# Roll of an 8192 x 8192 matrix: 31 of 128 row blocks copied by GpSimd's DMA ring

## The chip, the cores and the metric

The kernel runs on one core of one Trainium2 chip. The metric is the device time of one execution in microseconds; the median of the runs is given. Profiles are of one execution each.

## The reference

```python
def setup_inputs():
    return {"x": np.random.randn(8192, 8192).astype(np.float32), "shift": 100}

def reference(x, shift):
    return np.roll(x, shift, axis=1)
```

Every row of 8192 floats is rotated to the right by 100 places: column c of the result is column c - 100 of the input, and the first 100 columns are the input's last 100. Nothing is computed; 268.44 MB are read and 268.44 MB written.

## The kernel before

With s = 100, the kernel sets a = 256 (100 rounded up to a multiple of 128, plus 128) and g = a - s = 156. It splits each row at column a.

**The body** (lines 34 to 43): columns 256 to 8191 of the result are copied straight from HBM to HBM, 7936 floats or 31,744 bytes from a row. The 8192 rows are 128 blocks of 64 rows, and a block is seen as 16 groups (`e`) of 4 rows (`j`). One DMA copies row j of all 16 groups, so each of the 16 DMA engines gets one row. SP issues j = 0 and 2, ACT issues j = 1 and 3. In the last 4 blocks every row is cut at column `mid` = 4224, the middle of its 7936 columns, so that two DMAs of half rows stand where one was. SP's and ACT's DMAs are the hardware queues 1 and 10 of the profile. Each issuer has at most 4 DMAs in flight: it waits for its fourth last.

**The head** (lines 60 to 80): the first 256 columns of the result, of which 100 wrap around, go through SBUF. There are 16 stages of 512 rows, 4 rows on each of 128 partitions. For each stage GpSimd issues three loads on its software ring (queue 0): `t`, 3 runs of 1 KB for each partition, which span the end of one row and the start of the next; `h` with 100 floats (the wrapped end of the fourth row); and `h` with 156 floats (the start of the first row). VectorE puts the parts of `t` in their places in `h` with two copies. All stages have buffers of their own (`bufs=n_st`), so no load waits for a buffer. After the loads of all 16 stages GpSimd issues the 16 stores of `h` (line 80), 512 KB each. GpSimd has at most 8 DMAs in flight: each issue waits until the one eight before it has landed.

The order is the program's own: each issuer goes through its DMAs in the order of the loops, and body and head touch different columns, so no wait stands between them.

Of the kernel before, what the change touches and what calls it, by code (L numbers as in the profile page):

```python
# [1 line left out]

# [4 lines left out]


@with_exitstack
def kernel(  # L10
    ctx: ExitStack,
    tc: tile.TileContext,
    x: bass.AP,
    shift: int,
    out: bass.AP,
):
    nc = tc.nc
    n_rows, n_cols = x.shape
    s = shift % n_cols
    a = -(-s // 128) * 128  # L20
    if 0 < a <= 384 and a + 128 <= n_cols:
        a += 128
    g = a - s
    P = nc.NUM_PARTITIONS
    engines = [nc.sync, nc.scalar]
    n_chunks = 16
    rows = n_rows // n_chunks

    xm = x.rearrange("(c e j) w -> c j e w", e=16, j=4)
    om = out.rearrange("(c e j) w -> c j e w", e=16, j=4)
    if a < n_cols:
        blocks = n_rows // 64
        mid = (a + n_cols) // 256 * 128
        for c in range(blocks):
            parts = ((a, mid), (mid, n_cols)) if c >= blocks - 4 and a < mid else ((a, n_cols),)  # L40
            for j in range(4):
                for lo, hi in parts:
                    engines[j % 2].dma_start(out=om[c, j, :, lo:hi], in_=xm[c, j, :, lo - s:hi - s])
    if a == 0:
        return


    if a > 512:
        for i in range(n_chunks):
            r = slice(i * rows, (i + 1) * rows)  # L50
            nc.gpsimd.dma_start(out=out[r, :s], in_=x[r, n_cols - s:])
            if g > 0:
                nc.gpsimd.dma_start(out=out[r, s:a], in_=x[r, :g])
        return

    Q = 4  # L60
    n_st = n_rows // (P * Q)
    reads = ctx.enter_context(tc.tile_pool(name="reads", bufs=n_st))
    heads = ctx.enter_context(tc.tile_pool(name="heads", bufs=n_st))
    xt = x.rearrange("(k p q) c -> k p q c", q=Q, p=P)
    ot = out.rearrange("(k p q) c -> k p q c", q=Q, p=P)
    tiles = []
    for k in range(n_st):
        t = reads.tile([P, Q - 1, a], x.dtype)
        h = heads.tile([P, Q, a], x.dtype)
        lead = bass.AP(tensor=x.tensor, offset=(k * P * Q + 1) * n_cols - s,  # L70
                       ap=[[Q * n_cols, P], [n_cols, Q - 1], [1, a]])
        nc.gpsimd.dma_start(out=t[:], in_=lead, single_packet=True)  # L72
        nc.gpsimd.dma_start(out=h[:, Q - 1, :s], in_=xt[k, :, Q - 1, n_cols - s:], single_packet=True)  # L73
        nc.vector.tensor_copy(h[:, :Q - 1, :s], t[:, :, :s])  # L74
        if g > 0:
            nc.gpsimd.dma_start(out=h[:, 0, s:], in_=xt[k, :, 0, :g], single_packet=True)  # L76
            nc.vector.tensor_copy(h[:, 1:, s:], t[:, :, s:])  # L77
        tiles.append(h)
    for k, h in enumerate(tiles):
        nc.gpsimd.dma_start(out=ot[k, :, :, :a], in_=h[:], single_packet=True)  # L80


# [1 line left out]
_INS = ['x', 'shift']  # L84
_OUTS = [((8192, 8192), 'float32')]

_NUMBERS = {'shift': 100}


# [26 lines left out]
```

## Time and profile before

| | |
|---|---|
| median of 3 runs | 817.23 us (817.18 to 818.21) |
| span of the profiled execution | 813.9 us; the page has no other time of this execution, and the span lies 3.3 us below the median |
| GpSimd busy | 41.1 us, 68 instructions |
| VectorE busy | 12.0 us, 32 instructions |
| DMA of SP and of ACT | 248 of 496 KB and 16 of 248 KB each, median 12.5 and 5.9 us from issue to landing |
| head loads on the ring | 16 x 384, 78 and 50 KB, landing after 48.9, 41.9 and 47.2 us |
| head stores on the ring | 16 x 512 KB, landing after 102.9 us |
| first and last issue of a head store | 255.5 and 403.4 us |

The page gives for each DMA queue its packets, its megabytes, and the time of its packets as a share of the time of all 16 DMA engines. A copy from HBM to HBM counts once in the GB/s of a slice, although HBM is read and written. The time from issue to landing contains the waiting behind earlier DMAs of the same queue.

### The profile page before, as it was taken

The numbers are of one execution on the slowest core, as the hardware profiler recorded it, in microseconds if no ns is written. First come the engines' busy times: TensorE is split into PE (matmuls) and PEld (weight loads), VectorE is DVE, ScalarE is ACT, GpSimd is POOL, SyncE is SP. The second block draws the span as 40 slices with busy tenths as digits, with TensorE's granted clock in tenths as the row PEclk, the third lists the DMA queues.
The fourth block names the chain that finished last, engine by engine and source line by source line (L and its number), as shares of the span: only waits on it lengthen the run. The fifth ranks groups of instructions, "written<-read, shape, count | busy, mean of one in ns | idle before, by whom it ended". The sixth has DMA issues, their size and how long they took to land. (4 is left out here: it accounts for less than half of the span.)

```text
span 813.9 us, 689 instructions
## 1 busy us (share of the span) xinstructions
DVE 12.0 (1%) x32; POOL 41.1 (5%) x68
## 2 busy tenths in 40 slices
DVE  0000000000000000000000000000000000000000
POOL 2000011111000100000000000000000000000000
DMA  9999999999999999999999999999999999999998
GB/s 314 346 340 344 353 346 350 344 351 344 346 355 346 345 362 354 353 357 354 355 355 349 342 335 331 335 332 325 335 328 332 334 337 334 332 337 332 334 314 293
DMA packets 22277, 276.90 MB, mean 340 GB/s; under 512 B 9472, under 2 KB 9728, under 8 KB 13824
## 3 DMA queue, kind: packets, MB, share of 16 engines
q1 hardware_dynamic: 8448, 130.04, 45.9%
q10 hardware_dynamic: 8448, 130.04, 44.3%
q0 software_dynamic: 5376, 16.78, 8.9%
q14 instruction: 5, 0.04, 0.0%
HBM read 268.44 MB, written 268.44 MB: 660 GB/s over the span
## 5 line engine op out<-in xcount | busy, mean ns | idle before, releaser
L80 POOL DMA_DIRECT2D out_dram<-h x16 | 11.4, 713 | 139.5 <-DMA out_dram<-h 92.5
L76 POOL DMA_DIRECT2D h<-in_x_dram x16 | 8.6, 540 | 158.4 <-DMA t<-in_x_dram 158.4
L72 POOL DMA_DIRECT2D t<-in_x_dram x16 | 12.2, 760 | 32.1 <-DMA h<-in_x_dram 31.3
L73 POOL DMA_DIRECT2D h<-in_x_dram x16 | 8.9, 558 | 32.7 <-DMA h<-in_x_dram 32.7
L74 DVE COPY h<-t 128x300 f32<-128x300 f32 x16 | 5.9, 367 | 268.4 <-DMA t<-in_x_dram 268.4
L77 DVE COPY h<-t 128x468 f32<-128x468 f32 x16 | 7.5, 468 | 0.0
L97 POOL MEMSET const-float32-0.0<- 128x1 f32 x1 | 0.1, 98 | 0.2 <-issue 0.2
L97 POOL MEMSET const-bfloat16-1.0<- 128x1 bf16 x1 | 0.1, 101 | 0.0
L97 POOL MEMSET const-float32-1.0<- 128x1 f32 x1 | 0.1, 98 | 0.0
L97 POOL MEMSET const-uint8-127<- 128x1 uint8 x1 | 0.1, 98 | 0.0
## 6 DMA issues: line engine op xcount, KB each, us to landing
out_dram<-in_x_dram ACTq DMA_DIRECT2D x248, 496.0 KB, 12.5
out_dram<-in_x_dram SPq DMA_DIRECT2D x248, 496.0 KB, 12.5
out_dram<-h POOLq DMA_DIRECT2D x16, 512.0 KB, 102.9
t<-in_x_dram POOLq DMA_DIRECT2D x16, 384.0 KB, 48.9
out_dram<-in_x_dram SPq DMA_DIRECT2D x16, 248.0 KB, 5.9
out_dram<-in_x_dram ACTq DMA_DIRECT2D x16, 248.0 KB, 5.9
h<-in_x_dram POOLq DMA_DIRECT2D x16, 78.0 KB, 41.9
h<-in_x_dram POOLq DMA_DIRECT2D x16, 50.0 KB, 47.2
```

Source lines behind the costliest of these rows:

```text
L72: nc.gpsimd.dma_start(out=t[:], in_=lead, single_packet=True)
L73: nc.gpsimd.dma_start(out=h[:, Q - 1, :s], in_=xt[k, :, Q - 1, n_cols - s:], single_packet=True)
L74: nc.vector.tensor_copy(h[:, :Q - 1, :s], t[:, :, :s])
L76: nc.gpsimd.dma_start(out=h[:, 0, s:], in_=xt[k, :, 0, :g], single_packet=True)
L77: nc.vector.tensor_copy(h[:, 1:, s:], t[:, :, s:])
L80: nc.gpsimd.dma_start(out=ot[k, :, :, :a], in_=h[:], single_packet=True)
L97: nc = _bacc.Bacc("TRN2", target_bir_lowering=False, num_devices=1)
```

## The change

Blocks 3, 6, 9, ... 93, which are 31 of the 128, are taken out of SP's and ACT's loop. GpSimd copies them on its software ring, one DMA for a block: 64 rows, so 4 rows for each of the 16 engines. Two such DMAs are issued ahead of the head loads of each of the first 15 stages, one ahead of the sixteenth's. SP and ACT copy the other 97 blocks as before; the head's own instructions are unchanged, and stand behind the new DMAs in GpSimd's order.

```diff
         mid = (a + n_cols) // 256 * 128
+        lent = range(3, blocks - 32, 3) if 0 < a <= 512 else ()
         for c in range(blocks):
+            if c in lent:
+                continue
             parts = ((a, mid), (mid, n_cols)) if c >= blocks - 4 and a < mid else ((a, n_cols),)
...
     tiles = []
+    each = -(-len(lent) // n_st)
     for k in range(n_st):
+        for c in lent[k * each:(k + 1) * each]:
+            nc.gpsimd.dma_start(out=out[c * 64:(c + 1) * 64, a:].rearrange("(e j) w -> e j w", e=16),
+                                in_=x[c * 64:(c + 1) * 64, a - s:n_cols - s].rearrange("(e j) w -> e j w", e=16))
         t = reads.tile([P, Q - 1, a], x.dtype)
```

The new DMAs do not set `single_packet`; the head's DMAs do.

## The prediction

> **What bounds the kernel now.** I read the page first: slices, queues, bytes. Then the stretches of the span, then the list of DMA queues of three stretches that differ in what the GpSimd ring carries.
>
> The page: GpSimd and VectorE are almost idle, while the DMA engines are full in every slice.
>
> ```profile
> DVE 12.0 (1%) x32; POOL 41.1 (5%) x68
> DMA  9999999999999999999999999999999999999998
> DMA packets 22277, 276.90 MB, mean 340 GB/s; under 512 B 9472, under 2 KB 9728, under 8 KB 13824
> q1 hardware_dynamic: 8448, 130.04, 45.9%
> q10 hardware_dynamic: 8448, 130.04, 44.3%
> q0 software_dynamic: 5376, 16.78, 8.9%
> HBM read 268.44 MB, written 268.44 MB: 660 GB/s over the span
> ```
>
> A queue's numbers are packets, MB and its share of the time of 16 engines. The shares add up to 99.1%, so no engine waits for an issuer. Queues 1 and 10 (SP's and ACT's) have 8448 packets each for 4224 rows or half rows: a row of 31,744 bytes is one data packet and one completion packet of under 512 B. Queue 0 (GpSimd's ring) has 64 DMAs x 16 = 1024 completions and 4352 data packets, 17 for each stage and engine.
>
> The stretches (columns: length; VectorE; GpSimd; clock; DMA share; GB/s) show the rate falling when the ring runs dry near 503 us:
>
> ```profile
> 0.00:14.00 14.00, 0.00 (x0) 5.30 (x12) 1.00 0.87 307
> 14.00:500.00 486.00, 12.03 (x32) 35.85 (x56) 1.00 1.00 348
> 500.00:780.00 280.00, 0.00 (x0) 0.00 (x0) 1.00 0.99 333
> 780.00:814.00 34.00, 0.00 (x0) 0.00 (x0) 1.00 0.86 296
> ```
>
> That fall is no lost speed. A copy inside HBM counts once in GB/s but both reads and writes HBM; a head load or store touches HBM once. The queues of 40-240 us (head loads), 300-440 us (head stores) and 500-780 us (no ring), in this order:
>
> ```profile
> q1 hardware_dynamic: 1980, 31.49, 41.8%
> q10 hardware_dynamic: 1973, 31.27, 39.3%
> q0 software_dynamic: 2429, 6.59, 18.8%
> ...
> q1 hardware_dynamic: 1382, 21.87, 46.6%
> q10 hardware_dynamic: 1382, 21.91, 42.2%
> q0 software_dynamic: 1599, 5.82, 12.0%
> ...
> q10 hardware_dynamic: 2935, 46.54, 49.9%
> q1 hardware_dynamic: 2938, 46.64, 49.5%
> ```
>
> HBM traffic, twice queues 1 and 10 plus queue 0: (2 x 62.76 + 6.59)/200 us = 660.6 GB/s; (2 x 43.78 + 5.82)/140 = 667.0; 2 x 93.18/280 = 665.6. Three mixtures, one rate within 1%. I take the HBM at about 665 GB/s as the bound, and the 16 engines' full time as its shadow.
>
> **The change, part by part.** The span is 813.9 us, the median 817.23; I carry the 3.3 us between them unchanged.
>
> *Bytes.* The ring takes 31 x 64 rows = 62.98 MB; queues 1 and 10 keep 97/128 of 260.08 MB, 98.5 MB each. HBM traffic stays 536.88 MB: cost 0 while the rate stays about 665. What the new mixture does to the rate no row shows, since the ring never copies inside HBM here. Bounds: the rows 667.0 (-0.2%, -1.7 us) and 660.6 (+0.75%, +6 us). I take 665, as the added rows are the copies that the 500-780 stretch consists of.
>
> *Issue.* SP and ACT lose 124 DMA issues and completion waits between them. 31 GpSimd issues, at 540 to 760 ns by the rows of the head loads, are 17 to 24 us on an engine with 41.1 us of 813.9 busy: cost 0, hidden by the DMAs already in flight (8 of GpSimd's; it waits for the one eight back). Without that cover it would be the 24 us.
>
> *What queues behind.* The new copies stand ahead of each stage's head loads in the same ring, and GpSimd's later issues wait for them. So loads, VectorE copies and stores move later. Only the end matters: does the ring finish before the hardware queues? In packets for one DMA engine: a lent block is 4 rows and one completion, 5; a stage's loads are 9 + 3; a store is 8 + 1. Ring: 31 x 5 + 16 x 12 + 16 x 9 = 491. A hardware queue: 93 blocks x 2 x 2 + 4 split blocks x 2 x 2 x 2 = 404. The ring keeps up if it gets 491/404 = 1.215 packets for one of a hardware queue.
>
> The rows give what it gets. 40-240 us: 2429/1976 = 1.23. 300-440 us: 1599/1382 = 1.16. Over the ring's whole life (0-506 us: 5376 packets beside 4994 and 4985) 1.08, since engines drain it unevenly at the end. I take 1.10: a 31 KB row lasts longer than these ring packets, so a hardware queue that ran empty for a moment has been refilled before the ring's next turn. Ends: 1.23, and 1.0, strict alternation, below all three rows. The Trainium skill ("DMA: Bandwidth & Descriptors", Queues, rings and completion order) says that each DMA engine goes round its queues packet by packet; that alone would be 1.0, and this trace, with 1.08 to 1.23, shows a little more for the ring.
>
> At 1.10 the ring has sent 444 packets when the hardware queues end; 47 are left: 5.2 head stores of 0.524 MB. Alone they go at the engines' pace. In 300-440 us ring packets took 12.0% of 16 x 140 us for 5.82 MB: 21.6 GB/s an engine, 346 for 16, so a store takes 1.51 us, where at 665 GB/s of HBM it is worth 0.79. The loss is 0.72 us a store: 5.2 x 0.72 = +3.7 us. Ends: 9.7 stores (at 1.0), +7.0; none (from 1.215 on), 0.
>
> *Uneven engines.* The last store is issued at 403.4 us and the ring ends near 503, while its rate falls from about 440 on: some engines lag by a few stores. Behind the last row packet a lag of one to three stores costs 1.5 us each with the other engines empty. I take one, rounded down for the overlap: +1.3 us (0 to +4.5).
>
> *The end of before.* 780-814 us moves 296 GB/s where 333 was the rate: 34 x 37/333 = 3.8 us lost. Some 2 us of it are the empty last slices, which stay. Of the other 1.8 the ring's backlog fills half: -0.9 us (0 to -1.8).
>
> Sum: 817.2 + 3.7 + 1.3 - 0.9 = 821.3 us.
>
> **Rivals.**
>
> *No change, 817.2 us.* The ring gets its 1.215 or loses nothing by its tail, the HBM rate stays. For it: 1.16 and 1.23 stand on both sides of 1.215. The Trainium skill ("DMA: Bandwidth & Descriptors", Rules for kernel authors) says that spreading DMAs over SP, ACT and GpSimd does not raise bandwidth, because all run on the same 16 engines. The equal HBM rates agree. Against: balance is one point, and 1.215 is at the upper end of the rows.
>
> *Faster: the ring fills the ragged end, 814.4 us.* In 780-814 us the engines are 86% busy: 4.8 us of idle, 2.8 without the fixed 2 us. If every engine still has ring packets when its share of rows is done, that idle carries work: 817.2 - 2.8 = 814.4, and 812.7 with the 667.0 rate. It decides where the ring ends within about 3 us of the queues, at 1.19 to 1.24. A reason beyond the end would be fewer completions (one for four rows), but 780-814 us speaks against: mostly half rows, with twice as many completions a byte, took 10.07 MB in 85.7% of 34 us, 345.7 GB/s while busy, not less than 333/0.994 = 335.
>
> *Rows cut into small packets, 830 us.* All ring data packets seen here are small: the store's 32 KB an engine are 8 packets. Cut in the same way a 31 KB row would be 8 turns. Then the ring has 31 x 33 + 336 = 1359 packets, and by the end of the queues only about 444 are sent: 444/78 = 5.7 stages. The rest of the copies go alone at the HBM rate, and some 5.4 MB of loads and 8.4 of stores at 346 GB/s: 13.8 x (1/346 - 1/665) x 1000 = 19 us at worst, 13 if small transfers overlap with copies. Against: these small packets come from runs of at most 1 KB, while a hardware row is one packet. The Trainium skill ("DMA: Bandwidth & Descriptors", SWDGE vs HWDGE vs iDMA) gives up to 4096 B as the preferred packet; whether one long run is cut, no row here shows.
>
> *Worse mixture, 826 us.* The HBM rate drops to the lowest row's 660.6 while three streams run: about +5 us with a smaller tail.
>
> **How the numbers follow.** The ring last, 821.3 us (818.9 to 826): 0.45. No change: 0.17. Faster: 0.22. Cut rows: 0.08. Worse mixture: 0.08. About 0.2% (1.6 us) is what a measurement of this kernel can tell from no change. Slower is 0.45 + 0.08 + 0.08 = 0.61. The range 812 to 830 reaches past the faster case's 812.7 and to the cut rows.
>
> **What would show it.** Right: HBM traffic still 536.88 MB at 660 to 668 GB/s until the hardware queues end; queue 0 with 7856 packets (5376 + 31 x 80) and 79.8 MB, queues 1 and 10 with 6464; a hardware DMA lands in about 18 us instead of 12.5 (10 pairs of rows in a stage of 22 ring packets, 28 rows and 32 KB at 41.6 GB/s an engine = 43.5 us, so 4.35 us a pair where it was 3.06); the first store issued at 600 to 690 us instead of 255; near 805 us queues 1 and 10 stop, and 5 to 10 us of ring stores alone at 350 to 400 GB/s follow. Wrong: queue 0 idle before queues 1 and 10 end (balance), a packet count of queue 0 above 12,000 (cut rows), or an HBM rate in 100-600 us outside 658 to 670 (the mixture changes the bound).

## The result, and the profile after

The changed kernel takes 825.95 us (median of 4 runs, 825.32 to 828.61) where the kernel before takes 817.20 on the same chip: a ratio of 1.0109, 95% interval 1.0094 to 1.0124. It is slower by 8.8 us; the forecast was 4.1 us. The profiled execution took 825.32 us with a span of 823.5 us, 9.6 us longer than the span before. Between time and span lie 1.8 us here, and not the 3.3 us that were carried over from before; so the spans differ by more than the times.

The page of the changed kernel, in the lines that answer to those shown of before, with two lines of its DMA issues (KB each, median us from issue to landing):

```profile
DVE 12.0 (1%) x32; POOL 57.7 (7%) x99
DMA  9999999999999999999999999999999999999996
DMA packets 20789, 276.90 MB, mean 336 GB/s; under 512 B 7984, under 2 KB 8240, under 8 KB 12336
q1 hardware_dynamic: 6464, 98.55, 34.8%
q10 hardware_dynamic: 6464, 98.55, 33.1%
q0 software_dynamic: 7856, 79.76, 30.4%
HBM read 268.44 MB, written 268.44 MB: 652 GB/s over the span
...
out_dram<-in_x_dram SPq DMA_DIRECT2D x186, 496.0 KB, 17.4
out_dram<-in_x_dram POOLq DMA_DIRECT2D x31, 1984.0 KB, 66.6
```

The packet counts and the 17.4 us are those forecast (7856, 6464, about 18), so the change does what it says, and a lent row is one packet. But the shares add up to 98.3% where it was 99.1%: the engines have 14.0 us without a packet (1.7% of 823.5) instead of 7.3, and 809.5 us of packets instead of 806.6. Both grew; the shares are rounded to 0.1%, so each of these numbers is good to about 1 us.

The stretches of the changed kernel (length; VectorE; GpSimd; clock; DMA share; GB/s) show the end:

```profile
100.00:600.00 500.00, 9.02 (x24) 34.37 (x59) 1.00 0.99 336
600.00:700.00 100.00, 2.25 (x6) 8.64 (x13) 1.00 0.98 348
700.00:780.00 80.00, 0.00 (x0) 3.78 (x6) 1.00 1.01 354
780.00:800.00 20.00, 0.00 (x0) 1.91 (x3) 1.00 0.99 369
800.00:810.00 10.00, 0.00 (x0) 0.00 (x0) 1.00 1.00 369
810.00:823.50 13.50, 0.00 (x0) 0.00 (x0) 1.00 0.40 139
```

The last 13.5 us are 40% busy: 8.1 us idle, where 780 to 814 us of before had 4.8. The GB/s of that last stretch in 40 slices, and its queue 0, tell what is left there:

```profile
GB/s 165 118 94 0 12 71 470 282 153 636 71 329 329 401 141 94 423 212 517 470 141 106 59 0 47 0 24 24 24 24 24 24 24 24 0 0 0 0 24 0
q0 software_dynamic: 37, 0.13, 2.4%
```

Queue 0's 2.4% of 16 engines is 0.4 of one engine, and in the last slices 24 GB/s flow, the pace of one engine (the prediction's 21.6). One DMA engine is late on the ring; the other fifteen have finished it. The trace's records of landing show it too: a DMA has 16 of them, as many as there are engines, and in the ring's last three DMAs the sixteenth comes 13.4, 11.7 and 7.8 us after the fifteenth. At the start of the stretch queues 1 and 10 nearly stop (0 and 12 GB/s in two slices of 0.34 us) although they still have rows; their last packets end at 818.9 us, the ring's at 821.5 us.

The rest was lost on the way. Packets and queues of 160 to 480 us, first of the kernel before, then of the changed one:

```profile
q1 hardware_dynamic: 3164, 50.26, 45.4%
q10 hardware_dynamic: 3166, 50.32, 42.0%
q0 software_dynamic: 3465, 11.47, 13.1%
```

```profile
DMA packets 7132, 107.36 MB, mean 335 GB/s; under 512 B 2853, under 2 KB 2965, under 8 KB 3865
q0 software_dynamic: 2574, 34.96, 34.2%
q1 hardware_dynamic: 2275, 36.16, 33.2%
q10 hardware_dynamic: 2281, 36.22, 31.9%
```

HBM traffic before: (2 x 100.58 + 11.47)/320 us = 664.5 GB/s. After: the 3865 - 2853 = 1012 small data packets are head loads of 0.524 MB for every 144, so 3.7 MB; the other 31.3 MB of queue 0 are copies; (2 x (72.38 + 31.3) + 3.7)/320 = 659.6. That is 0.74% less, and the ring copies until about 670 us: 5.0 us. The traffic of the whole stretch from 0 to 670 us, counted in the same way, gives the same: 443.3 MB before and 440.1 MB after, 3.2 MB or 4.9 us.

Part of this is engines without a packet. In 160 to 480 us the shares sum to 100.5% before (over 100%, as the records of packets overlap a little) and to 99.3% after: 1.2%, or 3.8 of 320 us. How much of the 0.74% these gaps make, and how much slower rows, this page does not separate.

So the page accounts for 5.0 us in mid-run and 3.3 us of idle at the end, of 9.6; the other 1.3 us are in neither.

### The profile page after: what moved, and what is told of

Read it like the earlier page. It is cut to its first block, busy times and chain, and to the rows that moved or that the text cites. A ratio compares the mean times of both kernels' runs of the same rounds, so it can differ in the third digit from the quotient of the medians.

```text
span 823.5 us, 596 instructions
## 1 busy us (share of the span) xinstructions
DVE 12.0 (1%) x32; POOL 57.7 (7%) x99
## 3 DMA queue, kind: packets, MB, share of 16 engines
q1 hardware_dynamic: 6464, 98.55, 34.8%
q10 hardware_dynamic: 6464, 98.55, 33.1%
q0 software_dynamic: 7856, 79.76, 30.4%
## 4 chain that ended last, share of the span: by engine, by line
another core or an unknown queue 87%; DMA 6%; DVE 1%; POOL 1%; issue 1%; POOLq 0%; DVEq 0%; PEldq 0%
DMA t<-in_x_dram 6%; POOL out_dram L87 1%; DVE h L81 1%; DVE h L84 1%; POOL out_dram L73 0%; POOLq L118 0%; DVEq L118 0%; POOLq L87 0%; PEldq L118 0%
## 5 line engine op out<-in xcount | busy, mean ns | idle before, releaser
L73 POOL DMA_DIRECT2D out_dram<-in_x_dram x31 | 16.0, 516 | 176.6 <-DMA t<-in_x_dram 147.9
## 6 DMA issues: line engine op xcount, KB each, us to landing
out_dram<-in_x_dram SPq DMA_DIRECT2D x186, 496.0 KB, 17.4
out_dram<-in_x_dram ACTq DMA_DIRECT2D x186, 496.0 KB, 17.4
```

Source lines behind the costliest of these rows:

```text
L73: nc.gpsimd.dma_start(out=out[c * 64:(c + 1) * 64, a:].rearrange("(e j) w -> e j w", e=16), in_=x[c * 64:(c + 1) * 64, a - s:n_cols - s].r ...
```

## The experiments

Chips differ: the kernel before took 827.5 and 829.6 us in the first two groups, 816.2 and 815.8 in the last two. Every ratio is to the kernel before on the same chip.

**Fewer blocks.**

```diff
-        lent = range(3, blocks - 32, 3) if 0 < a <= 512 else ()
+        lent = range(3, blocks - 32, 6) if 0 < a <= 512 else ()   # 16 blocks; with 4: 24 blocks
```

> 16 blocks lent instead of 31, one ahead of each stage. Ring 16 x 5 + 336 = 416 packets an engine beside 464 of a hardware queue, so the ring should be done near 600 to 650 us. Theory L (most of the loss is one lagging DMA engine at the end of the ring, plus a slightly lower HBM rate while the ring copies): the tail is again that of before, only 16/31 of some 3 us of rate remain, 818.7 us (818 to 819.5). Rival M (the whole 8.75 us is the mixture, in proportion to the rows that the ring copies): 817.2 + 8.75 x 16/31 = 821.7 us.

> 24 blocks lent (every fourth up to 95). Ring 24 x 5 + 336 = 456 packets beside 432; at 1.2 packets for one it ends near 720 us, ahead of the hardware queues. Theory L: no ring tail, 24/31 of 3 us of rate, 819.6 us (818.5 to 820.5). Rival M: 817.2 + 8.75 x 24/31 = 824.0 us.

Measured: 16 blocks 1.0104 (1.0080 to 1.0128), 24 blocks 1.0090 (1.0066 to 1.0113). Theory L misses both times. Rival M's 824.0 us are 1.0083, inside the interval of 24 blocks, but its 821.7 us are 1.0055, far below that of 16 blocks: the loss did not shrink with the rows. With 16 blocks it is not the ring's end, since the ring's last packet ends at 772 us, some 60 us before the kernel does. With 24 blocks it can in part be the end: the ring was expected to be done near 720 us and ended at 828.7 us, together with the hardware queues (828.6), and the last 20 us are 77% busy against 86% with 16 blocks. Queues of 160 to 480 us with 16 blocks:

```profile
q1 hardware_dynamic: 2524, 40.16, 35.9%
q10 hardware_dynamic: 2524, 40.13, 34.4%
q0 software_dynamic: 2618, 24.86, 26.9%
```

They add up to 97.2%: engines without work in the middle of the run, 9 us in this stretch alone. With 24 blocks the sum is 99.3%.

**The same 31 blocks behind the head stores, whole or in rows.** Their DMAs ahead of the head loads are taken out.

```diff
     for k, h in enumerate(tiles):
         nc.gpsimd.dma_start(out=ot[k, :, :, :a], in_=h[:], single_packet=True)
+    for c in lent:          # whole; the other run: for j in range(4): om[c, j, :, a:] <- xm[c, j, ...]
+        nc.gpsimd.dma_start(out=out[c * 64:(c + 1) * 64, a:].rearrange("(e j) w -> e j w", e=16),
+                            in_=x[c * 64:(c + 1) * 64, a - s:n_cols - s].rearrange("(e j) w -> e j w", e=16))
```

> The same 31 blocks on the ring, but behind the head stores, so that the ring ends with 8 DMAs of 4 rows an engine in flight. Theory L: one engine is up to 8 DMAs behind, which are now 32 rows instead of 8 stores, so the end has one or few engines at work for 15 to 35 us: 835 to 850 us, with queue 0 alone at 25 to 50 GB/s in the last stretch. Rival of the prediction (the ring's backlog is even over the engines): copies inside HBM run at the HBM rate from one queue too, nothing is lost by the order, 817 to 826 us.

> As the run with the blocks last, but each lent block as four DMAs of one row an engine, like those of SP and ACT, so that 8 DMAs in flight are 8 rows an engine and not 32. Theory L: the lag is held to 8 rows of some 1.2 us, under 10 us of tail: 818 to 828 us, at least 10 us under the run with the blocks last. Rival (an even backlog, or a ring that is slow by itself): the same as the run with the blocks last, within 3 us.

Measured: whole blocks 1.0223 (1.0191 to 1.0256), rows 1.0057 (1.0035 to 1.0078); 847.4 and 831.7 us on a slower chip; by their ratios that would be 835.4 and 821.9 us beside the 817.2 us that the forecasts start from, both inside theory L. The last 20 us of the run with whole blocks, then of the one with rows:

```profile
819.70:839.70 20.00, 0.00 (x0) 0.00 (x0) 1.00 0.31 131
```

```profile
809.50:829.50 20.00, 0.00 (x0) 3.64 (x8) 1.00 0.79 258
```

The same bytes in the same order on each queue end with 31% or with 79% of the engines at work. In the records of landing the 16 engines of the very last DMA report within 41 us with whole blocks and within 3 us with rows. So the ring's backlog is not even over the engines, and it is the more uneven the more rows 8 DMAs hold. The rival is out. The order of the queues' ends differs as well: with rows SP's and ACT's queues end at 730 us and the ring goes on alone for 98 us, with whole blocks they end at 820 us.

**Rows instead of blocks with 16 lent, and deeper hardware queues.** The single change to the run with 16 blocks is the ring's `dma_start`, once for each j; in the next two, SP and ACT copy `[c, :, 2 * i:2 * i + 2]`, two rows an engine.

> The kernel before, unchanged, for a profile on the chip of these runs. All theories: the shares of its three queues add up to about 99%, as in the first profile, and the HBM traffic is within 1% of one rate in the stretches with and without the ring.

> 16 blocks lent as in the first run, but each as four DMAs of one row an engine, so that the ring's 8 DMAs in flight hold at most 8 rows of an engine instead of some 12 rows and more. Ring 16 x 8 + 336 = 464 packets beside 464 of a hardware queue. Theory D (the loss is engines that run dry: an engine that lags on the ring passes SP's and ACT's rows slower, their next DMA waits for all 16 engines, and the others have nothing left): the idle share at 160 to 480 us falls from 2.8% to under 1%, and the time from 1.010 to 1.002 to 1.006 of the kernel before. Rival H (the HBM is slower while three streams copy, idle engines are a by-product): 1.008 to 1.012 as with whole blocks.

> 16 blocks lent as whole DMAs, and SP and ACT copy two rows an engine in a DMA instead of one (the last four blocks as before), so that each hardware queue has 8 rows of an engine in flight instead of 4. Theory D: the other engines no longer run dry, the idle share at 160 to 480 us falls from 2.8% to under 1% and the time from 1.010 to 1.000 to 1.005. Rival H: 1.008 to 1.012.

> The kernel before with two rows an engine in a DMA of SP and ACT, nothing lent. It says how much of the run before it comes from the deeper queues alone. Theory D: little, since the three queues of before already fill 99% of the engines' time: 0.997 to 1.002. Rival H: 1.000.

The kernel before on this chip: span 826.9 us, shares 99.0%. Sixteen blocks as rows: 1.0030 (1.0015 to 1.0046). Its queues of 160 to 480 us:

```profile
q10 hardware_dynamic: 2616, 41.53, 38.3%
q1 hardware_dynamic: 2618, 41.59, 37.2%
q0 software_dynamic: 2886, 22.98, 23.9%
```

The sum is 99.4% instead of 97.2%, and two thirds of the loss are gone, as theory D said. Traffic at 160 to 480 us is still lower than before, though, 648.3 against 653.5 GB/s. The deeper hardware queues are a miss: 1.0133 (1.0111 to 1.0155) with nothing lent, 1.0218 (1.0193 to 1.0242) with 16 blocks. Two rows in a DMA of SP and ACT cost more than anything they could mend, so the second run decides nothing on D. No further run was made on why they cost that; the traces show one thing, which comes with the three streams below.

**The changed kernel again, smaller stores, pairs of rows.** The stores become `ot[k, :, 2 * i:2 * i + 2, :a]` for i in 0 and 1; the pairs are the ring's copies of 16 lent blocks, two rows an engine.

> The changed kernel unchanged, for its time and profile on the chip of these runs. Theory L+D (one engine is late on the ring at the end, and engines run dry in mid-run): 1.008 to 1.013 of before, the last 8 to 20 us with about one engine at work on queue 0, and the shares of the three queues add up to about 98.3%. Rival H (HBM slower while three streams copy): the same time, shares near 99%.

> The changed kernel with each head store as two of 256 KB, so that 8 DMAs in flight are 4 whole stores and not 8; nothing else differs (ring 507 packets instead of 491). Theory L: the late engine can be at most 4 stores behind instead of 6 or more, the end shortens by 2 to 4 us against the changed kernel. Rival H, or a loss in mid-run alone: within 1.5 us of the changed kernel, or slower by the 16 more packets.

> 16 blocks lent, each as two DMAs of two rows an engine: between whole blocks (1.0104) and single rows (1.003). Theory D: the time and the idle share at 160 to 480 us lie between the two, 1.004 to 1.009 and 1 to 2.5%. Rival (single rows did well for another reason, such as their turns in the queue): no order in it, at either end.

> The kernel before with each head store as two of 256 KB: what the smaller stores do by themselves. The ring ends near 500 us, far from the end. All theories: 0.998 to 1.002.

Measured: changed kernel 1.0128 (1.0110 to 1.0146), with half stores 1.0129 (1.0111 to 1.0147), pairs 1.0032 (1.0017 to 1.0046), before with half stores 0.9996 (0.9987 to 1.0005). The changed kernel's shares sum to 97.9% here, near what L+D said and not the 99% of H. Queue 0 in the last 10 us of the changed kernel, then of the one with half stores:

```profile
q0 software_dynamic: 86, 0.30, 7.7%
```

```profile
q0 software_dynamic: 640, 2.05, 58.5%
```

The first is few engines again (7.7% of 16 is 1.2): queues 1 and 10 end at 817.0 us, then two engines work on the ring until about 822 us (13% busy, 51 GB/s) and one until 826 us (6%, 25 GB/s). The late engine of the first profile is thus one or two, depending on the execution. With half stores they are gone, 9 engines work on the average; but the whole ring now ends behind the hardware queues, and 2.05 MB of even backlog take their place. Whether the 16 extra packets did this, or the half as many bytes in flight, is not separated. The time is the same. My 2 to 4 us did not come: I had left out the even backlog, which the prediction itself had priced. The pairs, expected between rows and blocks, are as good as rows, with 99.2% at 160 to 480 us; the order in rows that D wanted is not there, only whole blocks stand out.

**Three streams and nothing else.** Open was why the HBM rate is lower in mid-run. From 530 to 710 us the kernel before runs two streams of rows, and the versions with the blocks last run three; the fourth run moves the place of the lent rows.

```diff
-        lent = range(3, blocks - 32, 3) if 0 < a <= 512 else ()
+        lent = range(64, 95) if 0 < a <= 512 else ()
```

> The kernel before, for its profile on the chip of these runs: at 530 to 710 us only SP's and ACT's queues run. It is the measure for the next two, which have copies of GpSimd's ring as a third stream in the same stretch, and nothing small.

> 31 blocks on the ring behind the head stores, one row an engine in a DMA; at 530 to 710 us three streams of whole rows. Theory S (three streams lower the HBM rate by some 0.7%): MB in 530 to 710 us 0.5 to 1% below the kernel before. Theory D (only engines that run dry cost): the same MB within 0.3%.

> As the last, but four rows an engine in a DMA. Theory S: as the last. Theory D: the same MB as the kernel before while all engines have ring rows waiting (shares sum to 100%), the loss is all at the end.

> The changed kernel with blocks 64 to 94 lent instead of every third, so that the ring copies rows far from those of SP and ACT for most of the run. If it is where the third stream reads and writes that lowers the rate in mid-run, the HBM rate at 160 to 480 us moves by over 0.5% and the time by 3 us or more against 1.0109 to 1.0128; if not, 1.009 to 1.014 and the same rate.

The queues of 530 to 710 us of the kernel before, of the run with rows last, of the run with blocks last:

```profile
q10 hardware_dynamic: 1886, 29.94, 49.6%
q1 hardware_dynamic: 1887, 29.94, 49.4%
```

```profile
q0 software_dynamic: 1392, 22.22, 38.3%
q1 hardware_dynamic: 1420, 18.54, 31.0%
q10 hardware_dynamic: 1422, 18.65, 30.2%
```

```profile
q0 software_dynamic: 1059, 26.92, 45.8%
q1 hardware_dynamic: 1028, 16.32, 27.5%
q10 hardware_dynamic: 1018, 16.16, 26.8%
```

59.88, 59.41 and 59.40 MB: three streams move 0.8% less, and their shares sum to 99.5 and 100.1% against 99.0%. The rows last have half rows in this stretch, the blocks last have none. From 500 to 600 us all three have whole rows alone, and move 33.3, 32.8 and 33.0 MB. Where the three programs are still the same, from 20 to 250 us, their traffic (twice queues 1 and 10, plus queue 0) is within 0.3% of that of the kernel before: 152.2, 152.6 and 152.0 MB. So the lower rate is not a slower execution. No engine is short of work; a row of 31,744 bytes takes 1.51 us (0.990 x 2880 us / 1886 rows) with two streams and 1.53 and 1.54 us with three. Theory S holds in this stretch, D does not. The times, one execution each, go the same way: 815.6, 820.1 and 827.0 us.

GpSimd's ring is not slow by itself. In the run with rows last it is alone from 720 to 800 us:

```profile
q0 software_dynamic: 1669, 26.54, 99.5%
```

That is 332 GB/s, the 333 GB/s of the two hardware queues. But a third queue is not needed for the loss either. With two rows an engine in a DMA of SP and ACT and nothing lent, two queues move 16.16 MB in 735 to 785 us, where those of the kernel before on the same chip move 16.29 MB, 0.8% more, and the shares sum to 100.0% against 97.9%. So it may be the number of rows in flight that counts and not the number of queues. By the limits of the issuers, up to 8 rows an engine are in flight in the kernel before and with the ring alone, 16 in this run and with rows last, and 40 with blocks last. That fits, though 40 cost no more than 16; this is argued, no run was made for it.

With the lent blocks together the ratio is 1.0133 (1.0110 to 1.0155), and the traffic at 160 to 480 us is 659.9 GB/s, where it was 659.6: their place changes nothing that I could measure.

## Why the prediction was wrong, point by point

The direction was right and the size was not: 821.3 us forecast, 825.95 measured, inside the range of 812 to 830.

*What bounds the kernel.* That the HBM's traffic is the measure, and that the fall from 348 to 333 GB/s at 500 us is no lost speed, fits the runs: lending rows to keep the ring busy brought nothing back. The Trainium skill's rule ("DMA: Bandwidth & Descriptors", Rules for kernel authors) that spreading DMAs over SP, ACT and GpSimd does not raise bandwidth agrees with this. Of a cost the rule says nothing; here it was 1.0109.

*Bytes: the step that failed.* I took 0 for the new mixture, with +6 us as the far bound, and argued that the added rows are the copies of the two-queue stretch. But with the copies in three queues the traffic in mid-run was 0.74% lower, a term of some 5.0 us where the sum has 0. Two things can make it up, and their parts are not separated: gaps without a packet (3.8 of 320 us) and slower rows (0.8% less in the stretch with rows alone). Taken at the 660.6 row, the sum would have been 827.3 us, close to the measured time; but that row shows head loads beside two queues and says nothing of this mixture, so it would have been luck. What makes a row slower by 0.02 to 0.03 us is not settled: it is not the ring as such, nor, in that stretch, idle engines, and the place of the rows made no difference that could be measured. The number of queues and the number of rows in flight are the candidates left. The forecast's own sign for this step, a rate outside 658 to 670 GB/s in 100 to 600 us, did not show it: the rate was 659.7, and the band was wider than the loss.

*Issue and queueing.* Right. GpSimd's busy time grew by 16.6 us and cost nothing that the profile shows: its idle time is waiting for DMAs. The first store was issued at 647.5 us, inside 600 to 690.

*The end.* The sum of its three terms, +4.1 us, is near what the end costs (3.3 us more idle), but its parts were wrong. The ring got more turns than the 1.10 that I took: by 800 us it had sent 7696 of its 7856 packets beside 6146 and 6137, 1.25 for one, and fifteen engines had nothing of the even 5.2 stores left in the last microseconds. The 5 to 10 us of stores at 350 to 400 GB/s did not come. The 1.3 us for uneven engines was too small: one engine was some stores behind, alone at the last and, it seems, holding up the rows of SP and ACT before that, since their DMAs need all 16 engines. The half stores showed the forecast's own mechanism, an even backlog, and took the same time. The -0.9 us for filling the end of before came to nothing.

*The rivals.* No change and faster are out by the interval. Cut rows are out: 7856 packets. The rival "worse mixture" (826 us, given 0.08) is the one that came, together with the end; that its number is so close is in part luck, as it rests on the row of the head loads.

*What 16 blocks add.* They have no ring at the end and still cost 1.0%. A 0.8% lower rate over the 500 us in which 16 blocks are copied would be some 4 us (an estimate, from the stretch with rows alone); rows and pairs of rows cost 2.5 us by their ratios, so it is enough for theirs. Whole blocks cost 8.6 us, 6 us more, with engines idle in mid-run. That the wait of SP and ACT for a late engine makes them idle is argued from the runs with rows and pairs, not shown on its own.

No version beat the kernel before. The nearest, its half stores, is the same within 0.13%.

## What to carry to other kernels

When the DMA engines are full, as here, a third queue need not bring bandwidth and can cost some: count the traffic where it is limited (a copy inside HBM twice), and where no row shows the new mixture, carry the spread of the rows into the sum and not only into its range. A DMA counts as landed with the last of its 16 engines (in the changed kernel GpSimd's issue that waits comes 0.28 us after the sixteenth record of the DMA eight back, which can be over 60 us after the first), so several big DMAs in flight let one engine fall far behind; let the queue with the large DMAs end well before the others, or cut its DMAs small. Cutting adds packets to a queue that has its turns by packets, so count those too.

## What the runs showed of the hardware that I had not expected

- Three streams of 31,744-byte rows copy 0.8% less than two (59.4 against 59.9 MB in 180 us), with all engines at work. GpSimd's ring alone copies at 332 GB/s, like the two hardware queues.
- With 8 DMAs of four rows an engine in flight on the ring, the last 20 us were 31% busy and the 16 engines of the last DMA ended 41 us apart; with one row, 79% and 3 us.
- In a stretch with whole rows alone, queues took equal turns by packets, completions included: 685 of the ring beside 694 and 695 (rows last, 500 to 600 us).
- Two rows an engine in a DMA of SP and ACT instead of one, 992 KB instead of 496, made the kernel before slower: 1.0133.
- The kernel before took 815.8 to 829.6 us on four chips, a spread larger than the change itself.
